# RMS norm and projection on one core: pairs 12 to 14 moved into the loop's order, a new order for the head, output tiles in the weight tile, the last product in two halves

## The chip, the cores and the metric

The kernel runs on one core of one Trainium2 chip. The metric is the device time of one execution in microseconds, the median of several runs. A core has five engines that work side by side, each with its own instruction stream in a fixed order: TensorE (PE: matmuls and transposes, written to the eight banks of PSUM), VectorE (DVE), ScalarE (ACT), GpSimd (POOL) and SyncE (SP, which here issues DMA transfers). They wait for one another through semaphores.

## What is computed

```python
batch, n_heads, seq, head_dim = 8, 12, 1024, 64
dim = n_heads * head_dim                                  # 768
# x: (8, 1024, 768) float32; gamma: ones; w_qkv: (768, 2304) float32
def reference(x, gamma, w_qkv, eps):
    rms = np.sqrt(np.mean(x ** 2, axis=-1, keepdims=True) + eps)
    x_norm = x / rms * gamma
    return np.matmul(x_norm, w_qkv).astype(np.float32)
```

So 8192 rows of 768 are normalised and multiplied with a 768 x 2304 matrix.

## The kernel before, in words

The 8192 rows are 64 tiles of 128 rows. Tiles 0 to 3 are multiplied in the plain way: `mm` (L516) multiplies one 128 x 128 block of the transposed tile with 512 (at the end 256) columns of the bf16 weights, six times for a sum over 768. The other tiles are taken in pairs (pair p is tiles 2p and 2p+1, so pairs 2 to 31), and each pair is multiplied by a scheme of seven products in place of eight. The pair's 256 x 768 input is seen as 2 x 2 blocks, a chunk of 768 weight columns as 2 x 2 blocks of 384 x 384, and `product(p, c, i)` (L686) is product i of pair p and chunk c (0 to 2): three matmuls of 384 columns. The scheme needs four sums of input blocks for each pair (`osum`, L666, on DVE or POOL) and four differences of weight blocks for each chunk (`tsum`, L624, once for all pairs). Weights and inputs of this part are float16; the weights are scaled by a bound that `bound`, `fold`, `bound_tr`, `bound_top`, `bound_all` and `scales` find for each chunk. `bound_tr` and `bound_all` are small PE instructions with a small DVE instruction, `bound_top` (L590), between them.

The seven products of a chunk go to three PSUM banks, named a (products 1, 6, 7, 4 one after the other, added up in the bank), b (product 2) and c (5 and 3). Between two products on one bank its content is read out: `hold` (L693 on DVE, L695 on ACT) copies a bank to a buffer `pp`; `join` (L704, DVE) adds a bank to such a buffer and writes one of the four output quarters; `last` (L708, ACT) writes the fourth. PE can't go on with a bank until its reader is done. `pstore` (L714) sends an output tile of 128 x 768, or half of it, to DRAM.

A tile comes in by `load_x` (L437). In the plain part DVE casts it (`cast`), PE transposes it (`tr`, L480) and DVE or ACT copies the result to `xT` (`cp`); ACT computes the mean square (`stat`). In the pair part, `pstat` (ACT), `prms` (ACT) and `precip` (DVE) find the factor of each row, `pcast` (DVE, L648) writes the normalised tile in float16, and it is transposed either by a DMA (`pxbar`, on SP) or by PE and a copy (`ptr`, `pcp`). Weights come in 16 pieces (`load_w`, L442), which `conv` (L448 on DVE, L450 on ACT, L452 on POOL) converts to the bf16 weight tile `w_b`; `quad` makes the scaled float16 blocks from it. When all 12 of these blocks are made, `w_b` is not read again.

The order of all instructions is written out by hand. `PLAN` (from L19) is a list of 1028 operations with a time for each, and everything up to pair 14 is in it; `STEADY = 15` is the first pair of the loop at the end of the kernel, which gives each operation of pairs 15 to 31 a time in units of `SLOT` (0.4875, the time of one product) after `HEAD_END`. All operations are sorted by that time, and each engine gets its instructions in the order that results. The times are only keys for sorting; loop and list are mixed where their times overlap. In the list of before, pairs 13 and 14 are interleaved with each other, a product of one after a product of the other, and the products of pair 13 go on after `HEAD_END`.

Each kind of buffer comes from a pool of fixed size: 12 tiles `ot` for outputs, 6 `pp`, 4 `xb`, 10 `xT`, 3 sets of input sums, 8 PSUM banks. An instruction that writes into a buffer waits until the readers of what was in it are done, for an output tile until its store has landed.

Of the kernel before, what the change touches and what calls it, by code (L numbers as in the profile page):

```python
# [15 lines left out]
HEAD_END = 165.20  # L16
# [3 lines left out]
    (0.000, "load_x", 2), (4.040, "stat", 2), (4.041, "cast", 2, "DVE"), (4.042, "load_x", 1), (5.240, "stat", 1),  # L20
    (5.241, "load_x", 3), (5.242, "cast", 1, "DVE"), (5.243, "load_x", 0), (5.530, "recip", 2), (5.531, "load_w", 4),
    (5.532, "load_w", 1), (5.533, "load_w", 0), (5.534, "gamma_in"), (5.535, "idle", 6, 512), (5.536, "tr", 2),
    (8.470, "conv", 4, 5, "POOL"), (8.471, "cp", 2, "DVE"), (8.472, "cast", 3, "DVE"), (9.150, "conv", 1, 2, "POOL"),
    (9.151, "tr", 1), (9.152, "tr", 3), (9.153, "recip", 1), (9.154, "cast", 0, "DVE"), (9.155, "cp", 1, "ACT"),
    (9.156, "tr", 0), (9.157, "load_w", 3), (9.158, "cp", 0, "DVE"), (9.310, "mm", 1, 0, "5"), (9.311, "stat", 3),
    (9.526, "mm", 2, 0, "5"), (9.742, "mm", 0, 0, "5"), (9.743, "load_w", 2), (9.744, "load_w", 6),
    (9.745, "recip", 3), (9.990, "mm", 0, 0, "2"), (10.206, "mm", 1, 0, "2"), (10.451, "conv", 0, 0, "DVE"),
    (11.111, "conv", 3, 4, "DVE"), (11.112, "stat", 0), (11.113, "conv", 0, 1, "ACT"), (11.231, "bound", 0, 0, "ACT"),
    (11.541, "recip", 0), (11.772, "conv", 2, 3, "DVE"), (12.202, "cp", 3, "DVE"), (12.203, "mm", 1, 0, "01"),
    (12.204, "mm", 0, 0, "4"), (12.205, "mm", 2, 0, "4"), (12.206, "load_w", 7), (12.207, "mm", 1, 0, "4"),  # L30
    (12.342, "mm", 0, 0, "3"), (13.092, "conv", 6, 2, "DVE"), (13.093, "load_w", 5), (14.413, "conv", 7, 4, "POOL"),
    (14.414, "bound", 0, 1, "DVE"), (14.415, "mm", 1, 0, "3"), (14.416, "mm", 2, 0, "3"), (14.417, "load_w", 9),
    (14.418, "load_w", 8), (14.419, "conv", 6, 3, "ACT"), (14.420, "mm", 0, 0, "01"), (14.421, "mm", 2, 0, "012"),
    (14.422, "mm", 3, 512, "23"), (15.093, "conv", 7, 5, "POOL"), (15.094, "mm", 0, 512, "23"),
    (15.095, "mm", 1, 512, "23"), (15.096, "evac", 0, 0, "ACT"), (15.097, "load_w", 10), (15.098, "load_x", 4),
    (15.734, "conv", 5, 0, "DVE"), (17.054, "conv", 9, 3, "POOL"), (17.055, "evac", 1, 0, "ACT"),
    (17.056, "conv", 5, 1, "ACT"), (17.057, "bound", 0, 2, "ACT"), (17.734, "conv", 9, 2, "POOL"),
    (17.735, "bound", 1, 0, "DVE"), (18.414, "conv", 8, 1, "POOL"), (18.415, "mm", 3, 0, "012345"),
    (18.416, "mm", 1, 512, "45"), (18.417, "fold", 0), (18.418, "mm", 1, 512, "01"), (18.419, "mm", 3, 512, "01"),
    (18.420, "mm", 3, 512, "45"), (18.421, "load_x", 5), (18.544, "bound_tr", 0), (18.545, "evac", 1, 512, "ACT"),  # L40
    (18.664, "mm", 0, 512, "54"), (19.095, "mm", 0, 512, "01"), (19.096, "load_w", 15),
    (19.097, "evac", 3, 512, "ACT"), (19.098, "conv", 8, 0, "POOL"), (19.099, "bound_top", 0),
# [326 lines left out]
def kernel(  # L369
# [319 lines left out]
    def hold(p, c, bank, name, eng):  # L689
        o = PART[p, c, name] = parts.tile([P, CW], f32, name="pp")  # L690
        pb = PB[p, c, bank][:, :CW]
        if eng == "DVE":
            nc.vector.tensor_scalar(out=o, in0=pb, scalar1=SC[c], scalar2=None, op0=mult)  # L693
        else:
            nc.scalar.activation(out=o, in_=pb, func=AF.Copy, scale=SC[c], bias=0.0)  # L695

    def result(p, c, i, j):
        t = 2 * p + i
        if (t, "s", c) not in OUT:
# [107 lines left out]
```

## Time and profile before

| | us |
|---|---|
| three runs | 355.93, 356.56, 357.06 (median 356.56) |
| the profiled execution | 356.93 |
| its span, first to last instruction | 354.8 |
| PE busy | 343.6 |
| DVE busy | 267.8 |
| ACT busy | 243.7 |
| POOL busy | 116.9 |

The mean granted clock of TensorE was 0.995. The durations that matter, by group of instructions: a join 613 ns on DVE, a hold 616 on DVE and 582 on ACT, `last` 577 on ACT, `pcast` 678 on DVE, a weight difference 785 on DVE, an input sum 925 to 938 on POOL. A DMA store of 384 KB takes a median of 4.6 us to land, one of 192 KB 2.3 us. The DMA queues moved 117.8 MB, 332 GB/s over the span.

In a line of the timeline or chain, the first number is the start in us from the first instruction and the second how long it took; "pm L686 x87" is 87 instructions of line 686 that write the tile pm (PSUM). Square brackets give the idle time of that engine just before, and what ended it. In a table of stretches, each column is the busy time of PE, PE's weight loads, DVE, ACT and POOL in that stretch with the number of instructions in brackets, then the granted clock, the busy share of the DMA engines and GB/s.

### The profile page before, as it was taken

What the parts mean: (1) busy time and instruction counts of PE and PEld (TensorE: products, weight loads), DVE (VectorE), ACT (ScalarE), POOL (GpSimd) and SP (SyncE); (2) the same over time, 40 slices, a digit from 0 to 9 for tenths busy, and PEclk for the clock granted to TensorE, in tenths of its full rate; (3) what the DMA queues carried; (4) which work ended last, traced back from release to release, by engine and by line L of the source; (5) the groups of instructions that cost most, each with busy time, mean ns of one, the idle gap of its engine ahead of it and who ended that gap; (6) DMA issues with size and microseconds to landing.
All of it is one profiled execution on the core that took longest, in us unless ns stands there. A gap on an engine that the chain in (4) does not pass through costs nothing.

```text
span 354.8 us, 6638 instructions
## 1 busy us (share of the span) xinstructions
PE 343.6 (97%) x2113; PEld 203.6 (57%) x2113; DVE 267.8 (75%) x504; ACT 243.7 (69%) x498; POOL 116.9 (33%) x135
## 2 busy tenths in 40 slices
PE   5999999999999999999899999999999999999995
PEld 2446566666665656655456566565666656566562
DVE  3689999788778878887676868677777867676663
ACT  6798989878885557656457667676767677665543
POOL 0396444222233303650254080613407061444000
PEclk9899999999999999999999999999999999999999
DMA  7999999999998999999999999999999999987565
GB/s 267 389 381 307 360 416 345 400 347 378 324 393 254 303 361 329 282 350 396 320 332 371 255 380 353 366 334 304 365 360 383 333 327 343 313 305 262 208 266 222
DMA packets 80493, 117.80 MB, mean 332 GB/s; under 512 B 43590, under 2 KB 45388, under 8 KB 80460
## 3 DMA queue, kind: packets, MB, share of 16 engines
q1 hardware_dynamic: 80448, 117.40, 99.1%
q8 instruction: 16, 0.26, 0.3%
q14 instruction: 17, 0.14, 0.1%
q10 hardware_dynamic: 12, 0.00, 0.0%
HBM read 32.25 MB, written 75.50 MB: 304 GB/s over the span
## 4 chain that ended last, share of the span: by engine, by line
PE 54%; DVE 1%; ACT 0%; issue 0%
PE pm L686 54%; DVE ot L704 1%; DVE xb L648 0%; ACT ot L708 0%; DVE pp L693 0%
## 5 line engine op out<-in xcount | busy, mean ns | idle before, releaser
L686 PE MATMUL pm<-wq,su 128*128 128x384 f16 x1080 | 204.9, 326 | 0.8 <-DVE ot L704 0.8
L704 DVE SCALAR_TENSOR_TENSOR ot<-pm,sc,pp 128x384 f32<-128x384 f32 x270 | 156.6, 613 | 47.6 <-PE pm L686 42.3
L695 ACT ACTIVATE pp<-pm,sc 128x384 f32<-128x384 f32 x203 | 114.0, 582 | 75.3 <-PE pm L686 71.9
L686 PE MATMUL pm<-wq,xT 128*128 128x384 f16 x810 | 160.9, 326 | 1.7 <-DVE ot L704 1.5
L686 PEld LDWEIGHTS <-su 128*128 128x128 f16 x1080 | 105.2, 98 | 70.1 <-issue 1.2
L686 PEld LDWEIGHTS <-xT 128*128 128x128 f16 x810 | 79.1, 98 | 54.7 <-issue 2.6
L666 POOL TENSOR_TENSOR su<-xT 128x384 f16<-128x384 f16 x51 | 46.3, 925 | 154.3 <-PE pm L686 84.9
L708 ACT ACTIVATE ot<-pm,sc 128x384 f32<-128x384 f32 x90 | 51.8, 577 | 25.5 <-PE pm L686 24.9
L693 DVE TENSOR_SCALAR pp<-pm,sc 128x384 f32<-128x384 f32 x67 | 40.9, 616 | 23.5 <-PE pm L686 23.0
L634 ACT ACTIVATE sq<-x_t 128x768 bf16<-128x768 f32 x60 | 50.3, 838 | 0.1
L648 DVE TENSOR_SCALAR xb<-x_t,rstd 128x768 f16<-128x768 f32 x60 | 40.3, 678 | 0.4
L666 POOL TENSOR_TENSOR su<-su,xT 128x384 f16<-128x384 f16 x27 | 25.3, 938 | 26.5 <-DVE su L666 14.6
L666 POOL TENSOR_TENSOR su<-xT,su 128x384 f16<-128x384 f16 x27 | 25.2, 935 | 10.0 <-DVE su L666 6.7
L516 PE MATMUL pm<-w_b,xT 128*128 128x512 bf16 (+1 forms) x120 | 26.2, 375 | 0.4 <-POOL w_b L452 0.4
L516 PEld LDWEIGHTS <-xT 128*128 128x128 bf16 x120 | 11.8, 101 | 12.5 <-issue 2.7
L452 POOL TENSOR_SCALAR w_b<-wq,g_sb 128x512 bf16<-128x512 f32 (+1 forms) x14 | 9.1, 662 | 14.0 <-DMA wq<-in_w_qkv_dram 14.0
L618 POOL TENSOR_SCALAR wq<-w_b,inv 128x1152 f16<-128x1152 bf16 x9 | 11.2, 1261 | 4.9 <-DVE inv L602 4.9
L634 ACT ACTIVATION_READ_ACCUMULATOR sq<-x_t 128x1 f32 x60 | 11.7, 195 | 0.0
L624 DVE TENSOR_TENSOR wq<-wq 128x1152 f16<-128x1152 f16 x12 | 9.2, 785 | 0.0
L573 DVE TENSOR_REDUCE bnd<-w_b 128x1 f32<-128x1536 bf16 x5 | 8.7, 1747 | 0.3 <-ACT w_b L450 0.3
L638 ACT ACTIVATE rms<-ssq,eps_sb 128x2 f32<-128x2 f32 x30 | 8.8, 294 | 0.0
L534 ACT ACTIVATE ot<-pm,rstd 128x512 f32<-128x512 f32 x10 | 6.6, 684 | 1.1 <-PE pm L516 1.0
(48 smaller groups left out, 79.3 us busy)
## 6 DMA issues: line engine op xcount, KB each, us to landing
out_dram<-ot SPq DMA_DIRECT2D x178, 384.0 KB, 4.6
x_t<-in_x_dram SPq DMA_DIRECT2D x64, 384.0 KB, 5.4
wq<-in_w_qkv_dram SPq DMA_DIRECT2D x10, 512.0 KB, 9.1
out_dram<-ot SPq DMA_DIRECT2D x8, 512.0 KB, 9.3
wq<-in_w_qkv_dram SPq DMA_DIRECT2D x4, 256.0 KB, 6.8
xT<-xb SPq DMA_TRANSPOSE x49, 5.0
wq<-in_w_qkv_dram SPq DMA_DIRECT2D x2, 384.0 KB, 9.7
out_dram<-ot SPq DMA_DIRECT2D x4, 192.0 KB, 2.3
```

The costliest lines, as they stand in the source:

```text
L452: nc.gpsimd.tensor_scalar(out=o, in0=i, scalar1=g, scalar2=1.0, op0=mult, op1=mult)
L516: nc.tensor.matmul(out=PM[t, n0][:, :nl], lhsT=XT[t][:, ko, :], rhs=w_b[:, ko, n0:n0 + nl], start=(b == 1), stop=(b == KO))
L618: nc.gpsimd.tensor_scalar(out=o, in0=quad_view(c, q), scalar1=INV[c], scalar2=1.0, op0=mult, op1=mult)
L624: (nc.vector if eng == "DVE" else nc.gpsimd).tensor_tensor(out=new_quad(c, q), in0=i0, in1=i1, op=sub)
L634: nc.scalar.activation(out=sq, in_=X[t], func=AF.Square, accum_out=SS[p][:, t % 2:t % 2 + 1])
L648: nc.vector.tensor_scalar(out=XB[t], in0=X[t], scalar1=SS[t // 2][:, t % 2:t % 2 + 1], scalar2=None, op0=mult)
L666: (nc.vector if eng == "DVE" else nc.gpsimd).tensor_tensor(out=block(p, q), in0=block(p, x), in1=block(p, y), op=op)
L686: nc.tensor.matmul(out=PB[k][:, :CW], lhsT=block(p, a)[:, ko, :], rhs=WQ[c, b][:, ko, :], start=(first and ko == 0), stop=(ko == KO // 2 - ...
L693: nc.vector.tensor_scalar(out=o, in0=pb, scalar1=SC[c], scalar2=None, op0=mult)
L695: nc.scalar.activation(out=o, in_=pb, func=AF.Copy, scale=SC[c], bias=0.0)
L704: nc.vector.scalar_tensor_tensor(out=result(p, c, i, j), in0=PB[p, c, bank][:, :CW], scalar=SC[c], in1=PART[p, c, held], op0=mult, op1=add)
L708: nc.scalar.activation(out=result(p, c, 1, 0), in_=PB[p, c, "a"][:, :CW], func=AF.Copy, scale=SC[c], bias=0.0)
```

## The change

The list `PLAN` is replaced by another. It holds the same 1028 operations; about eighty of them stand on another engine (DVE, ACT or POOL) than before, and nearly all have another place. `HEAD_END` is 169.75 in place of 165.20; `STEADY` stays 15. In the new list pairs 12, 13 and 14 follow one another, with the products of a pair in the order that the loop uses, each chunk's products 7 and 4 among the first products of the next chunk. The third chunk of pair 4 stood in the list's times 131 to 142 among pairs 10 to 12; now its seven products are spread from 149 to 173, the last three of them around the first products of the loop. The two kernels' starts, shortened:

```diff
 PLAN = [
-    (0.000, "load_x", 2), (4.040, "stat", 2), (4.041, "cast", 2, "DVE"), (4.042, "load_x", 1), (5.240, "stat", 1),
-    (5.241, "load_x", 3), (5.242, "cast", 1, "DVE"), (5.243, "load_x", 0), (5.530, "recip", 2), (5.531, "load_w", 4),
-    (5.532, "load_w", 1), (5.533, "load_w", 0), (5.534, "gamma_in"), (5.535, "idle", 6, 512), (5.536, "tr", 2),
+    (0.000, "load_x", 1), (1.160, "load_x", 3), (4.040, "stat", 1), (4.041, "cast", 1, "DVE"), (4.042, "load_x", 2),
+    (4.043, "gamma_in"), (4.044, "idle", 6, 512), (5.030, "cast", 3, "DVE"), (5.031, "load_w", 2), (5.260, "tr", 1),
+    (5.820, "cp", 1, "DVE"), (5.821, "stat", 3), (6.820, "stat", 2), (6.821, "load_w", 3), (6.822, "load_x", 0),
+    (6.823, "tr", 3), (6.824, "load_w", 4), (7.480, "conv", 2, 3, "POOL"), (7.481, "load_w", 1),
+    (7.482, "cast", 2, "DVE"), (7.483, "tr", 2), (8.141, "conv", 3, 4, "ACT"), (8.142, "cp", 2, "DVE"),
+    (8.320, "mm", 1, 0, "3"), (8.660, "mm", 2, 0, "3"), (8.921, "mm", 1, 0, "4"), (9.131, "stat", 0),
+    (10.331, "cp", 3, "ACT"), (10.332, "mm", 2, 0, "4"), (10.333, "conv", 4, 5, "POOL"), (10.334, "cast", 0, "DVE"),
+    (10.335, "tr", 0), (10.631, "mm", 2, 0, "5"), (10.847, "mm", 1, 0, "5"), (10.848, "load_w", 0),
...
-    (51.670, "product", 3, 2, 2), (51.671, "tsum", 2, "t2", "DVE"), (52.488, "hold", 3, 2, "a", "p1", "ACT"),
-    (58.464, "product", 4, 0, 6), (58.465, "tsum", 2, "t4", "DVE"), (58.466, "join", 2, 2, 1, 1, "a", "p5"),
+    (51.967, "tsum", 2, "t1", "DVE"), (51.968, "tsum", 2, "t2", "POOL"), (51.969, "pcast", 9),
+    (59.829, "pstore", 3, 1, 0), (59.830, "tsum", 2, "t4", "POOL"), (59.831, "product", 4, 0, 5),
```

And the seam of the list and the loop:

```diff
-    (163.257, "hold", 13, 1, "a", "u2", "DVE"), (163.742, "product", 13, 1, 7), (164.229, "product", 14, 2, 2),
-    (164.632, "join", 13, 1, 1, 1, "a", "p5"), (164.717, "product", 14, 1, 7), (165.204, "product", 14, 2, 6),
-    (165.404, "join", 14, 1, 1, 1, "a", "p5"), (165.692, "product", 14, 2, 3),
-    (166.179, "product", 13, 2, 6), (166.867, "hold", 13, 2, "a", "u2", "ACT"), (166.868, "product", 13, 1, 4),
...
-    (171.054, "product", 13, 1, 3), (171.254, "last", 13, 2), (171.742, "join", 13, 1, 0, 1, "c", "u2"),
+    (169.265, "product", 14, 1, 4), (169.618, "join", 14, 2, 0, 1, "c", "u2"), (169.953, "last", 14, 1),
+    (170.308, "pstore", 14, 2, 0), (170.728, "pstore", 14, 1, 1), (170.729, "product", 14, 2, 7),
+    (170.730, "join", 14, 2, 1, 1, "a", "p5"), (170.731, "product", 4, 2, 2), (170.732, "product", 4, 2, 4),
+    (170.990, "join", 4, 2, 0, 0, "b", "p1"), (171.215, "product", 14, 2, 4), (171.415, "last", 4, 2),
+    (172.055, "pstore", 4, 2, 1), (172.056, "last", 14, 2), (172.057, "product", 4, 2, 3),
```

Output tiles: from pair 4 on, the outputs of chunk 2, and in even pairs also those of chunk 1 of the second tile, are written into slots of `w_b`, nine slots of 768 float32 used in turn. The last chunk of the last pair: product 4 is done as two products of 192 columns, the first half is written out by DVE and stored by SP, the second half by ACT and stored from ACT's queue.

```diff
+    spare = []
     def result(p, c, i, j):
         t = 2 * p + i
         if (t, "s", c) not in OUT:
-            OUT[t, "s", c] = outp.tile([P, 1024], f32, name="ot")
+            if p >= 4 and (c == 2 or (c == 1 and i == 1 and p % 2 == 0)):
+                s = 2 * CW * (len(spare) % (KO * N // (4 * CW)))
+                spare.append((t, c))
+                OUT[t, "s", c] = w_b.rearrange("p k n -> p (k n)").bitcast(f32)[:, s:s + 2 * CW]
+            else:
+                OUT[t, "s", c] = outp.tile([P, 1024], f32, name="ot")
         return OUT[t, "s", c][:, CW * j:CW * (j + 1)]
...
+    def end_piece(p, c, h):
+        w = CW // 2
+        k = (p, c, "a")
+        a, b = PRODUCTS[4]
+        for ko in range(KO // 2):
+            nc.tensor.matmul(out=PB[k][:, w * h:w * (h + 1)], lhsT=block(p, a)[:, ko, :], rhs=WQ[c, b][:, ko, w * h:w * (h + 1)],
+                             start=False, stop=(ko == KO // 2 - 1), skip_group_check=True)
+
+    def end_out(p, c, h):
+        w = CW // 2
+        t = 2 * p + 1
+        o, pb = result(p, c, 1, 0)[:, w * h:w * (h + 1)], PB[p, c, "a"][:, w * h:w * (h + 1)]
+        if h == 0:
+            nc.vector.tensor_scalar(out=o, in0=pb, scalar1=SC[c], scalar2=None, op0=mult)
+        else:
+            nc.scalar.activation(out=o, in_=pb, func=AF.Copy, scale=SC[c], bias=0.0)
+        n0 = 2 * CW * c + w * h
+        (nc.sync if h == 0 else nc.scalar).dma_start(out=of[t * P:(t + 1) * P, n0:n0 + w], in_=o)
...
                 when(9.6, pstore, p, c, 0, 0)
-                when(9.7, last, p, c)
-                when(10.6, pstore, p, c, 1, 0)
+                when(8.5, end_piece, p, c, 0)
+                when(8.6, end_piece, p, c, 1)
+                when(9.7, end_out, p, c, 0)
+                when(9.8, end_out, p, c, 1)
```

In the program that is built, PE raises its semaphore once for the two halves, after the sixth matmul. DVE's output of the first half waits for that count, and ACT's output of the second half waits for DVE's. The orders of DVE, ACT and POOL in the list's part are new; their sums of work are compared in the prediction.

## The prediction

> **What bounds the kernel now.** I read the page first, then busy time in stretches of 10 us, then the chain that ended last, then the timelines of the first 20 us, of 148 to 180 us and of the end.
>
> ```profile
> span 354.8 us, 6638 instructions
> PE 343.6 (97%) x2113; PEld 203.6 (57%) x2113; DVE 267.8 (75%) x504; ACT 243.7 (69%) x498; POOL 116.9 (33%) x135
> ...
> 140.00:150.00 10.00, 10.00 (x63) 6.05 (x62) 8.50 (x17) 7.04 (x16) 5.05 (x6) 1.00 1.16 294
> 150.00:160.00 10.00, 9.51 (x60) 5.59 (x59) 8.69 (x15) 5.49 (x11) 5.98 (x7) 1.00 1.06 336
> 160.00:170.00 10.00, 9.21 (x56) 5.35 (x55) 6.99 (x14) 6.70 (x15) 0.00 (x0) 1.00 1.02 384
> 170.00:180.00 10.00, 9.04 (x56) 5.25 (x54) 7.14 (x12) 3.20 (x6) 3.56 (x4) 1.00 1.13 320
> 180.00:190.00 10.00, 10.00 (x64) 5.99 (x63) 6.86 (x13) 6.73 (x14) 5.76 (x7) 1.00 1.02 362
> ```
>
> TensorE (PE) is the bound. From 20 to 150 us and from 180 to 350 it has no idle time; a full stretch issues 63 or 64 matmuls. Only 150 to 180 falls short (60, 56, 56). The chain says where:
>
> ```profile
> 153.49 14.47 PE pm L686 x87
> ...
> 169.12 0.54 DVE ot L704
> 169.66 0.04 issue
> 169.70 0.66 PE pm L686 x3
> ...
> 170.94 0.63 DVE ot L704
> 171.57 0.04 issue
> 171.62 6.02 PE pm L686 x36
> 177.64 0.02 issue
> 177.66 0.59 ACT ot L708
> 178.25 0.04 issue
> 178.29 171.29 PE pm L686 x1053
> ```
>
> From 178.29 on, 1053 matmuls take 171.29 us: 0.1627 each, 0.488 a product of three. Before that, PE waits for evictions of PSUM banks. An idle mark understates a wait, since a matmul's modelled end lies 0.16 past its slot, so I take starts from the timeline: three matmuls at 152.34 should be followed at 152.83, and the next starts at 153.49 (0.66); likewise 164.69 to 164.85 (0.16), 168.75 to 169.70 (0.95), 170.68 to 171.62 (0.94), 177.95 to 178.29 (0.34). Sum 3.05 us. All five lie in pairs 12 to 14 and their seam with the regular loop.
>
> Two more losses stand at the ends.
>
> ```profile
> 9.38 1.36 POOL L452 TENSOR_SCALAR w_b<-wq,g_sb 128x512 bf16<-128x512 f32 x2 [7.95 <-DMA wq<-in_w_qkv_dram]
> 10.12 10.05 PE L516 MATMUL pm<-w_b,xT 128*128 128x512 bf16 x38 [0.44 <-POOL w_b L452]
> 13.75 5.92 PEld L516 LDWEIGHTS <-xT 128*128 128x128 bf16 x28 [0.24 <-issue]
> 350.27 0.65 PE L686 MATMUL pm<-wq,xT 128*128 128x384 f16 x3 [0.22 <-DVE ot L704]
> 350.96 0.58 ACT L708 ACTIVATE ot<-pm,sc 128x384 f32<-128x384 f32 x1 [1.27 <-PE pm L686]
> ```
>
> The first real matmul waits until 10.12 for weights; up to 13.7 the weight loads of 128x512 matmuls follow 0.43 us apart, after that 0.216: half clock, about 1.8 us lost. At the end, the last product waits 0.38 for a join of its bank (349.89 to 350.27), then come 0.69 to ACT's output, 0.58 for it, and a store.
>
> [...]
>
> **The change, part by part.** The instructions of the head are the same in number: the list of operations differs only in engines and order. Only the last product changes on PE, from three matmuls to six of half width[...]. Sums are against the profiled execution, 356.93 us (span 354.8 and 2.1 around it); the median shown is 0.37 lower, and I subtract that at the end.
>
> *Pairs 12 to 14 in the regular pattern, loop start moved behind them.* In the built order I counted PE work between a product that fills a bank and the instruction that overwrites it. The end of the old kernel gives the price: product at 348.92, join 349.61 to 350.23, next writer 350.27. So 0.86 us of other PE work must lie between; 0.49 lay there and 0.38 was lost. In the old head two places have too little: 0.00 (the 0.94 wait) and 0.49 (the 0.34). The other three have 0.97 or 1.46, with DVE or ACT queued behind casts of x and holds. In the new order nothing from pair 12 to the loop is under 0.97, with the loop's own succession of holds and joins, which from 180 to 349 costs no wait. I count -3.05, and +0.1 for pair 4's third chunk, whose products and joins still sit at the seam.
>
> *Start.* The x order is 1, 3, 2, 0 and two weight pieces come ahead of x 0. Landings by cumulative KB, seen from what waited for them: 384 at 3.85, 768 at 4.82, 1152 at 7.59, 1536 at 8.55, 2560 at 11.33, 3584 at 13.98. In the new order piece 2 ends at 1408 KB: about 8.2, its conversion on POOL 0.69, first matmul 8.9 (before 10.12). But PE then runs out: piece 4 (2304 KB) lands at 10.65 and is ready at 11.4, piece 0 (3072 KB) at 12.65. Between, four matmuls by 10.1, then six at half clock, 11.4 + 6 x 0.43 = 13.97; from there 0.2157 each, so the 30th starts at 13.97 + 19 x 0.2157 = 18.07. Before, 38 are done at 20.10, so the 30th starts at 18.16. Gain 0.1. If the clock stayed full, piece 0 would decide (12.65 + 0.72 + 0.05): gain 0.6. If the window after 13.7 is half too, each such window costs 1.7. I take -0.1. One new wait: the first scale's bound_all now has two matmuls (0.43) behind bound_tr instead of four; transpose 0.22, DVE's 0.28 and two handoffs of 0.06 need 0.62. +0.1; the head's ordinary matmuls queue behind it.
>
> *Rest of the head.* Instructions times mean, by stretches of PE work: from 0 to 50 us of it DVE has 53.9 us (before 54.5), ACT 56.3 (56.7), sums above 50 that the old kernel bore without a wait because neighbours overlap by about 0.06. From 50 to 100 DVE rises from 45.9 to 49.5, ACT falls from 44.1 to 40.3. Tight: the joins of pair 2 behind four weight differences on DVE (trace about 44 to 50), and one join (pair 4, first chunk, bank b) with 0.49 us to the transposes of tile 15 that take a bank; if DVE is free there, 0.38 is lost unless another release hides it. Two weight differences move to POOL, a form that the trace lacks: at least 1.26 (POOL's one-input pass over 1152), at most 3 x 0.925 = 2.78[...]; four sums are queued behind. For all of this +0.4; from 0 to 2.
>
> *Nine output tiles in spent weights.* The old trace shows DVE and ACT waiting for stores of their output tile 0.4 us each in all, outside the chain's PE waits. Nothing. Such a tile waits for the store of nine uses earlier: at five uses in two pairs of 21 x 0.488 = 10.2 us each, over 30 us ago.
>
> *Last product in halves.* PE raises its count once, after the sixth matmul; so DVE's half starts no earlier than the whole did, and ACT's half waits for DVE's. Extrapolated from 256 and 384 columns: DVE 478, 616, so 0.41; ACT 470, 577, so 0.42. From PE's count: 0.41 + 0.05 + 0.42 = 0.88 against 0.58, +0.3. The last store is half as large: stores took 1.8 to 2.8 to land and the end of this one overlaps the drain of those ahead; I take -0.1 (0 to -0.3), while ACT's issue may be slower (0.57 for gamma, 0.33 on SP). Together +0.2, from -0.1 to +0.5. Nothing is queued behind. The 0.38 wait stays.
>
> Sum: -3.05 + 0.1 - 0.1 + 0.1 + 0.4 + 0.2 = -2.35; 356.93 - 2.35 - 0.37 = 354.2.
>
> **Rivals.**
> - *Cleaner*: clock full at the start (-0.6), no wait in the head, the tail even: -3.05 + 0.1 - 0.6 + 0.1 = -3.45, 353.1. For it: PE has 1.2 us of work between 6.9 and 10.3 where it had 0.85. [...]
> - *The head takes it back*: a wait of about 1 us where DVE's differences and joins meet, and others of 0.4 to 0.9 at tile 15 and at POOL's differences: 2.4 instead of 0.4, 356.2. For it: DVE is 9.8 of 10 busy at 40 to 60, and the whole order is new. Against: the old kernel bore the same sums without one wait.
> - *Slower*: the start starves PE between 9 and 13.5 us, and the clock stays half for two windows more, to 20.5. Price 2 x 1.7: 357.6, above the old median. It decides once two windows are lost. For it: from 10.1 to 11.4 PE has six transposes only. Against: from 11.4 PE never stops, and the old kernel warmed after one such window.
>
> **How the numbers follow.** Forecast 0.45 (353.4 to 355.3), cleaner 0.20, head 0.21, slower 0.14. The range 352.9 to 356.5 leaves out the slower case and edges of the others. 0.3% of the median is 1.07 us, about what a measurement of this kernel can tell from no change. Faster than 355.5: cleaner 0.20, forecast 0.43, a quarter of the head case 0.05: 0.68. Slower than 357.6: most of that case, 0.11. Same 0.21.
>
> **What would show it.** Right: all stretches of 150 to 180 with 63 or 64 matmuls; the unbroken PE run begins before 60 us; the 30th ordinary matmul starts near 18.1; ACT's last output starts after DVE's and ends about 1.5 us after the last product's start. Wrong: PE waits on L714 or L718 between 40 and 80 us that sum to over 1.5; half clock after 14 us; a tail shorter than before.

## The result, and the profile after

The changed kernel takes 355.14 us in the median of 4 runs (355.04 to 355.33); the kernel before, run beside it, 356.25 us (355.66 to 357.06). The ratio is 0.9968, with a 95% interval of 0.9946 to 0.9990. Run once more, with 22 runs against 45, it was 355.26 against 356.07 us, ratio 0.998 (0.9967 to 0.9993). So the change is worth 0.8 to 1.1 us, less than half of the 2.35 of the prediction's sum. The profiled execution of the changed kernel took 355.04 us, span 353.0; that of the kernel before 356.93, span 354.8. From one profile to the other that is -1.89 us.

The time lies inside the range on record, 0.9 us above the 354.2 forecast, but the terms are not those of the sum. First the table by stretches of the changed kernel (stretch; its length, busy time of PE and matmuls; granted clock; DMA share; GB/s):

```profile
40.00:60.00 20.00, 19.55 (x132) 1.00 1.03 381
60.00:80.00 20.00, 19.58 (x134) 1.00 1.07 372
80.00:150.00 70.00, 70.00 (x436) 1.00 1.04 341
150.00:160.00 10.00, 9.83 (x62) 1.00 1.09 277
160.00:170.00 10.00, 10.00 (x63) 1.00 1.08 390
170.00:180.00 10.00, 9.59 (x60) 1.00 1.10 329
180.00:340.00 160.00, 160.00 (x987) 1.00 0.98 326
```

The three stretches from 150 to 180 us, which held 9.51, 9.21 and 9.04 us of busy PE before, are almost full: the five old waits are gone. But there are two new ones among them, and two more between 40 and 80 us, where the old kernel had none. The timeline shows what stands ahead of each. First the one at 41.60 us (start; length; engine, line, operation, tiles; in brackets the idle time before and what ended it):

```profile
40.79 1.14 PE L689 MATMUL pm<-wq,su 128*128 128x384 f16 x6
40.99 0.75 DVE L627 TENSOR_TENSOR wq<-wq 128x1152 f16<-128x1152 f16 x1
41.66 0.15 DVE L583 TENSOR_REDUCE bmax<-bnd 128x1 bf16<-128x3 f32 x1
41.72 1.13 DVE L714 SCALAR_TENSOR_TENSOR ot<-pm,sc,pp 128x384 f32<-128x384 f32 x2
...
42.38 0.22 PE L588 MATMUL pm<-ident,bmax 128*1 128x128 bf16 x1 [0.45 <-DVE ot L714]
```

PE's small transpose for the third scale needs a PSUM bank. A join of pair 2 frees it, and DVE comes to that join only at 41.72, behind a weight difference (L627). The last of the six matmuls before it started at 40.79 + 5 x 0.163 = 41.60 and takes 0.163, so 0.62 us are lost by 42.38; 0.09 of that is lost before such a transpose without a wait for a bank too. The other three, in the same view:

```profile
70.55 0.91 POOL L669 TENSOR_TENSOR su<-xT 128x384 f16<-128x384 f16 x1 [3.65 <-DMA xT<-xb]
70.81 1.59 DVE L651 TENSOR_SCALAR xb<-x_t,rstd 128x768 f16<-128x768 f32 x2
71.43 1.14 PE L689 MATMUL pm<-wq,xT 128*128 128x384 f16 x6
72.33 0.61 DVE L714 SCALAR_TENSOR_TENSOR ot<-pm,sc,pp 128x384 f32<-128x384 f32 x1
72.99 0.48 PE L689 MATMUL pm<-wq,su 128*128 128x384 f16 x2 [0.42 <-DVE ot L714]
...
150.28 1.78 POOL L669 TENSOR_TENSOR su<-xT 128x384 f16<-128x384 f16 x2 [2.21 <-PE pm L689]
151.30 1.19 DVE L651 TENSOR_SCALAR xb<-x_t,rstd 128x768 f16<-128x768 f32 x1
153.45 1.63 PE L689 MATMUL pm<-wq,su 128*128 128x384 f16 x9
154.04 0.62 DVE L651 TENSOR_SCALAR xb<-x_t,rstd 128x768 f16<-128x768 f32 x1
154.59 1.13 DVE L714 SCALAR_TENSOR_TENSOR ot<-pm,sc,pp 128x384 f32<-128x384 f32 x2
155.24 0.65 PE L689 MATMUL pm<-wq,xT 128*128 128x384 f16 x3 [0.17 <-DVE ot L714]
...
176.26 0.91 POOL L669 TENSOR_TENSOR su<-xT,su 128x384 f16<-128x384 f16 x1
176.45 1.13 DVE L651 TENSOR_SCALAR xb<-x_t,rstd 128x768 f16<-128x768 f32 x1
177.67 1.67 PE L689 MATMUL pm<-wq,su 128*128 128x384 f16 x9
178.56 0.60 DVE L651 TENSOR_SCALAR xb<-x_t,rstd 128x768 f16<-128x768 f32 x1
179.08 1.66 DVE L714 SCALAR_TENSOR_TENSOR ot<-pm,sc,pp 128x384 f32<-128x384 f32 x3
179.74 0.65 PE L689 MATMUL pm<-wq,xT 128*128 128x384 f16 x3 [0.41 <-DVE ot L714]
```

By starts, from the last matmul of the group before to the next one and less one matmul of 0.163, these are 0.58 us (72.24 to 72.99), 0.33 (154.75 to 155.24) and 0.57 (179.01 to 179.74). In all three a cast of x (L651) stands ahead of the join in DVE's queue, and a cast shortly before took 1.06 to 1.19 us where 0.61 is usual: each time POOL had begun a sum (L669) 0.15 to 0.27 us before it. (In the second group the second sum of the pair is the one that counts: it starts at 151.15.) In this trace 6 of the 60 casts took over 0.8 us, and each ended 0.41 to 0.42 us after the end of the sum that was running when it started (70.55 + 0.91 = 71.46, and the cast at 70.81 took 1.06 and ended at 71.87). What in the chip makes the cast late was not shown.

Start and end of the changed kernel, from the timeline of PE and of the last engines:

```profile
8.66 1.19 PE L519 MATMUL pm<-w_b,xT 128*128 128x512 bf16 x4 [0.57 <-POOL w_b L455]
10.89 1.46 PE L519 MATMUL pm<-w_b,xT 128*128 128x512 bf16 x6 [0.36 <-POOL w_b L455]
12.89 5.99 PE L519 MATMUL pm<-w_b,xT 128*128 128x512 bf16 x26 [0.54 <-ACT w_b L453]
...
348.31 0.66 PE L725 MATMUL pm<-wq,xT 128*128 128x192 f16 x6 [0.22 <-DVE w_b L714]
349.00 0.42 DVE L733 TENSOR_SCALAR w_b<-pm,sc 128x192 f32<-128x192 f32 x1 [0.22 <-PE pm L725]
349.46 0.42 ACT L735 ACTIVATE w_b<-pm,sc 128x192 f32<-128x192 f32 x1 [1.73 <-DVE w_b L733]
```

In this execution no ordinary matmul ran at half rate: six take 1.46 us together. The two halves at the end are evicted one behind the other, as predicted. The sum between the two profiles:

| part | predicted | between the profiles | from |
|---|---|---|---|
| five waits at 150 to 178 gone | -3.05 | -3.05 | starts of matmuls |
| new waits there | +0.1 | +0.90 | 0.33 + 0.57 |
| new waits in the head | +0.4 | +1.20 | 0.62 + 0.58 |
| start, up to 40 us | -0.1 + 0.1 | -1.01 | the rest up to the last product, which starts at 348.31 instead of 350.27 |
| last product's start to the end of the span | +0.2 | +0.19 | 4.71 against 4.52 |
| around the span | 0 | -0.09 | 2.04 against 2.13 |
| sum | -2.35 | -1.86 | -1.89 by the times, the difference is rounding |

### The profile page after: what moved, and what is told of

It reads as the page before. It is cut to its first block, busy times and chain, and to the rows that moved or that the text cites. A ratio compares the mean times of both kernels' runs of the same rounds, so it can differ in the third digit from the quotient of the medians.

```text
span 353.0 us, 6601 instructions
## 1 busy us (share of the span) xinstructions
PE 342.4 (97%) x2113; PEld 203.6 (58%) x2116; DVE 267.1 (76%) x503; ACT 242.6 (69%) x497; POOL 123.5 (35%) x137
## 4 chain that ended last, share of the span: by engine, by line
PE 91%; DVE 3%; DMA 2%; SPq 1%; issue 1%; ACT 0%
PE pm L689 84%; PE pm L519 6%; DMA wq<-in_w_qkv_dram 2%; DVE wq L627 1%; PE pm L674 1%; DVE ot L714 1%; DVE xb L651 1%; SPq L445 1%; SPq L440 0%; DVE xT L459 0%; ACT w_b L453 0%; PE pm L725 0%; DVE w_b L714 0%; DVE su L669 0%; ACT pp L698 0%
## 5 line engine op out<-in xcount | busy, mean ns | idle before, releaser
L714 DVE SCALAR_TENSOR_TENSOR ot<-pm,sc,pp 128x384 f32<-128x384 f32 x172 | 100.2, 612 | 27.0 <-PE pm L689 24.3
L669 POOL TENSOR_TENSOR su<-xT 128x384 f16<-128x384 f16 x50 | 46.1, 938 | 147.0 <-PE pm L689 71.0
L714 DVE SCALAR_TENSOR_TENSOR w_b<-pm,sc,pp 128x384 f32<-128x384 f32 x98 | 58.4, 615 | 23.6 <-PE pm L689 22.4
L651 DVE TENSOR_SCALAR xb<-x_t,rstd 128x768 f16<-128x768 f32 x60 | 39.8, 665 | 0.4
L718 ACT ACTIVATE ot<-pm,sc 128x384 f32<-128x384 f32 x48 | 27.4, 576 | 12.2 <-PE pm L689 11.0
L669 POOL TENSOR_TENSOR su<-xT,su 128x384 f16<-128x384 f16 x28 | 26.2, 936 | 23.1 <-PE pm L689 14.7
L718 ACT ACTIVATE w_b<-pm,sc 128x384 f32<-128x384 f32 x41 | 23.5, 576 | 13.7 <-PE pm L689 13.5
L669 POOL TENSOR_TENSOR su<-su,xT 128x384 f16<-128x384 f16 x26 | 24.9, 958 | 14.3 <-PE pm L689 10.0
L519 PE MATMUL pm<-w_b,xT 128*128 128x512 bf16 (+1 forms) x117 | 25.2, 357 | 1.6 <-POOL w_b L455 0.9
L455 POOL TENSOR_SCALAR w_b<-wq,g_sb 128x512 bf16<-128x512 f32 (+1 forms) x16 | 11.6, 731 | 12.6 <-DMA wq<-in_w_qkv_dram 12.6
L576 DVE TENSOR_REDUCE bnd<-w_b 128x1 f32<-128x1536 bf16 x6 | 10.3, 1748 | 0.6 <-ACT w_b L453 0.3
L621 POOL TENSOR_SCALAR wq<-w_b,inv 128x1152 f16<-128x1152 bf16 x8 | 9.7, 1224 | 1.8 <-DVE inv L605 1.8
L453 ACT ACTIVATE w_b<-wq,g_sb 128x512 bf16<-128x512 f32 (+1 forms) x12 | 7.8, 666 | 3.3 <-DMA wq<-in_w_qkv_dram 3.1
```

Of the source, the lines that this page charges most:

```text
L455: nc.gpsimd.tensor_scalar(out=o, in0=i, scalar1=g, scalar2=1.0, op0=mult, op1=mult)
L519: nc.tensor.matmul(out=PM[t, n0][:, :nl], lhsT=XT[t][:, ko, :], rhs=w_b[:, ko, n0:n0 + nl], start=(b == 1), stop=(b == KO))
L576: nc.vector.tensor_reduce(out=o, in_=v, axis=mybir.AxisListType.XY, op=amax, apply_absolute_value=True)
L621: nc.gpsimd.tensor_scalar(out=o, in0=quad_view(c, q), scalar1=INV[c], scalar2=1.0, op0=mult, op1=mult)
L651: nc.vector.tensor_scalar(out=XB[t], in0=X[t], scalar1=SS[t // 2][:, t % 2:t % 2 + 1], scalar2=None, op0=mult)
L669: (nc.vector if eng == "DVE" else nc.gpsimd).tensor_tensor(out=block(p, q), in0=block(p, x), in1=block(p, y), op=op)
```

## The experiments

Each kernel ran beside the kernel before on the same chip (42, 45 and 27 runs of it in the three groups, medians 355.94, 356.07 and 356.11 us). All of them compute the full output.

### The waits for joins

**Casts one join earlier.** If a sum holds up the cast, the cast should be started ahead of the sum:

```
- when((-45, -57)[odd] + 4.5 * i, pcast, t)
+ when((-45, -57)[odd] + 4.5 * i - {31: 0.98, 36: 0.3}.get(t, 0), pcast, t)
```

> The changed kernel with two casts of x on DVE (tiles 31 and 36) each moved ahead of the one join that stood before it; nothing else on any engine. Theory (a cast waits for a GpSimd sum that started just before it): in the changed kernel these casts took 1.19 and 1.13 us instead of 0.61, started 0.15 and 0.19 us after a sum on POOL, and the PE waits of 0.33 us at 154.75 and 0.57 at 179.01 follow from them. Started one join earlier they are ahead of the sum, take about 0.61, both PE waits go, and the span falls by 0.9 us (0.5 to 1.0). Rival (DVE has too many joins of the held-back chunks in these pairs): the work on DVE is the same in number, so both waits stay within 0.15 us of what they were and the span is unchanged.

Measured: 354.92 us in the median of 9, ratio 0.9973 (0.9960 to 0.9987). The wait at 179 fell from 0.57 to 0.16, that at 154.7 stayed at 0.33. The moved casts met the sum that stood one further ahead: tile 31 took 0.84 us, tile 36 0.95, and now the next cast, tile 32, met a sum too (0.97). Neither theory holds as written. The collision is not removed by moving a cast by one place, since four sums of 0.91 us or more follow one another closely on POOL. The span of 351.9 is only in part the edit's: in this profile the wait at 41 us, which the edit doesn't touch, was 0.11 instead of 0.62.

**The two head waits by order.** A weight difference goes behind the two joins, and a product that opens a bank behind one that does not:

```
- (40.165, "tsum", 1, "t3", "DVE")       (71.862, "product", 5, 1, 5)
+ (41.566, "tsum", 1, "t3", "DVE")       (72.476, "product", 5, 1, 5)
```

The hold that reads this product moved along, from 72.360 to 72.800.

> The changed kernel with the first two waits of the head attacked by order: a weight difference on DVE (chunk 1, t3) moved behind the two joins of pair 2 that stood after it, and on PE product 5 of pair 5, chunk 1 moved behind product 3 of chunk 2. Theory (these are order waits for a join that frees a PSUM bank): the waits of 0.62 us at 41.60 and 0.58 at 72.24 fall to 0.1 or less each, span lower by 1.0 us (0.6 to 1.2). Rival (DVE is simply full there, so that the next instruction in its queue is late instead): waits of the same sum appear within 5 us behind the old places, span unchanged within 0.2.

Measured: 354.73 us in the median of 10, ratio 0.9969 (0.9960 to 0.9978). The first wait is gone (its transpose costs its usual 0.09), the second is 0.15, and nothing came in their place; 0.33 and 0.57 are unchanged. No cast was held up near the second wait in this profile; in three later ones with the same order, where one took 1.27 to 1.34 us, it is 0.28 to 0.36. The theory holds for the waits: about 1.0 us less in the profile. The medians differ by only some 0.5 (354.73 against the 355.26 of the next run), and why they don't show the whole was not settled.

**The changed kernel again.** No edit.

> The changed kernel itself, unedited, beside the others on the same chip. Theory (its waits for joins differ from run to run, because it matters to a fraction of a microsecond which of a DVE pass and a GpSimd sum starts first): the span's waits in the head, 0.62 and 0.58 us in the first profile, come out between 0.1 and 0.8 each; those at 154.7 and 179.0 stay at 0.33 and 0.57; time 355.1 (354.3 to 355.8). Rival (the waits are fixed by the order): all four within 0.05 us of the first profile.

Measured: 355.26 us in the median of 22 (354.19 to 356.81). In this profile the waits are 0.62, 0.83, 0.32 and 0.57. Over the five other profiles that keep the head's order of the changed kernel (the runs with earlier casts, old tail, extra sum, late products and all outputs in ot), the first wait was 0.11, 0.29, 0.15, 0.61 and 0.61, the second 0.78, 0.78, 0.39, 0.75 and 0.42. So the head's waits differ from execution to execution, while 0.33 and 0.57 come back within 0.02 in three of these six profiles. The theory holds in kind; the median time is as expected.

What they differ by can be read in the same profiles. Where one of the weight differences ahead of the first wait took 1.47 us instead of 0.75 (the first profile and three of these), the wait is 0.61 or 0.62. In the three others all of them took 0.75, a sum on POOL beside them took 3.63 us instead of 1.36, and the wait is 0.11, 0.15 and 0.29. The second wait is 0.39 in the profile with the extra sum, where no cast was held up ahead of its join and DVE waited for PE: so much the order costs with DVE free. In the others it follows the cast ahead: 0.42, 0.58, 0.75, 0.78 and 0.83 us where that took 0.90, 1.06, 1.23, 1.27 and 1.32. And the wait at 179 is 0.78 and 1.26 in two profiles, where the cast just ahead of the join was held up too, to 0.82 and 1.30 us: 0.21 and 0.69 more than 0.57, as much as that cast took beyond 0.61. So, with the order unchanged, these two waits of PE grow by as much as a cast on DVE is held up.

**Holds on ACT besides.** With the head reordered, DVE is relieved of one hold ahead of each late join:

```
- (151.941, "hold", 13, 1, "c", "p5", "DVE")
+ (151.941, "hold", 13, 1, "c", "p5", "ACT")
- when(2.1, hold, p, c, "c", "p5", "DVE" if c < 2 else "ACT")
+ when(2.1, hold, p, c, "c", "p5", "DVE" if c < 2 and (p, c) != (15, 1) else "ACT")
```

> The reordering of the two head waits (as in the run of that name: a weight difference behind two joins, one product behind another), and besides the holds of bank c of pairs 13 and 15, chunk 1, on ACT instead of DVE, so that DVE has 0.55 us less to do ahead of the late joins. Theory (PE waits because the join of bank a stands late in DVE's queue; ACT idles 0.9 and 1.4 us there): the waits of 0.33 at 154.7 and 0.57 at 179.0 fall to under 0.1 each; all waits for joins between 40 and 180 us sum to 0.3 or less instead of 2.10; span 351.2 to 351.6, time 354.0 in the median, 1.0 under the changed kernel's. Rival (other instructions become late in their place): the sum stays above 1.0 and the time within 0.4 us of the changed kernel's.

Measured: 353.86 us in the median of 6 (353.54 to 354.18), ratio 0.9936 (0.9920 to 0.9952): 1.4 under the changed kernel beside it. The wait at 179 fell to 0.09. The head kept 0.35 about 72 us and 0.13 at 43, and the wait at 154.4 stayed at 0.32, so that the sum is 0.9 and not 0.3. Why the last of these stayed, the timeline says:

```profile
152.98 0.91 POOL L669 TENSOR_TENSOR su<-xT,su 128x384 f16<-128x384 f16 x1
153.29 1.02 DVE L651 TENSOR_SCALAR xb<-x_t,rstd 128x768 f16<-128x768 f32 x1
...
154.88 0.81 PE L689 MATMUL pm<-wq,xT 128*128 128x384 f16 x4 [0.16 <-DVE ot L714]
```

Without the hold, the cast of tile 32 started earlier, at 153.29, met the sum of 152.98 and took 1.02 us; it ended at 154.31, 0.42 after the sum. The relief was eaten by the 0.41 us that the sum cost the cast.

**The collision by itself.** A needless subtraction on GpSimd is put ahead of a cast in the regular loop, where the changed kernel waits nowhere:

```
+ def extra(p):
+     v = OUT[2 * p, "s", 0][:, :576]
+     nc.gpsimd.tensor_tensor(out=scratch, in0=v, in1=v, op=sub)
...
+ if p % 2 and 17 <= p <= 29 and c == 0:
+     when(6.6, extra, p)
```

> The changed kernel with one needless GpSimd subtraction of 576 f32 columns into a scratch tile in each odd pair from 17 to 29 (seven in all), started by the join that stands two instructions ahead of a cast of x on DVE in the regular loop, where the changed kernel has no PE wait at all; one output buffer fewer makes room for the scratch. Theory (a cast waits for a GpSimd pass that started before it): the seven casts take 0.9 to 1.3 us instead of 0.61, each ends about 0.42 us after the subtraction does, and PE waits of 0.2 to 0.6 us appear before product 4 of chunk 0 in these pairs, together 1.4 to 4 us; span higher by as much. Rival (DVE's own work alone makes joins late): casts at 0.61, no new wait, span unchanged within 0.3.

Measured: 357.27 us in the median of 12, 2.0 above the changed kernel beside it; ratio to the kernel before 1.0031 (1.0015 to 1.0047). The first of them, in pair 17 (the lines of this kernel stand five further down, L694 is the product, L656 the cast, L719 the join):

```profile
198.34 1.15 POOL L635 TENSOR_TENSOR scratch<-ot 128x576 f16<-128x576 f32 x1 [16.58 <-DVE ot L719]
198.73 1.63 PE L694 MATMUL pm<-wq,su 128*128 128x384 f16 x9
198.98 0.93 DVE L656 TENSOR_SCALAR xb<-x_t,rstd 128x768 f16<-128x768 f32 x1
199.83 1.66 DVE L719 SCALAR_TENSOR_TENSOR ot<-pm,sc,pp 128x384 f32<-128x384 f32 x3
200.48 0.81 PE L694 MATMUL pm<-wq,xT 128*128 128x384 f16 x4
```

In the changed kernel, where PE's nine matmuls start at 198.75, the same cast and join read:

```profile
199.00 0.61 DVE L651 TENSOR_SCALAR xb<-x_t,rstd 128x768 f16<-128x768 f32 x1
199.52 1.14 DVE L714 SCALAR_TENSOR_TENSOR ot<-pm,sc,pp 128x384 f32<-128x384 f32 x2
```

The subtraction ends at 199.49, the cast at 199.91; the join behind it starts 0.31 later than the 199.52 of the changed kernel, and PE's nine matmuls, over at 198.73 + 9 x 0.163 = 200.19, are followed at 200.48: a wait of 0.29. All six pairs from 17 to 27 show the same, 0.93 us for the cast and 0.29 for PE, 1.74 together; pair 29 has no cast left at that place, which the expectation overlooked. The rival falls: DVE has not one instruction more. Not all of the 2.0 us is the subtraction's: at 178.3 the profile has 1.26 instead of 0.57, where the cast of tile 37 met a sum and took 1.30. The missing output buffer shows at 47 to 50 us, where DVE waits three times for a store of `ot` (1.5 us), and PE 0.2 us at 50.6; in pairs 17 to 27 nothing waits for a store.

**Casts behind the joins.** Back to holds on DVE; the cast stays in its neighbourhood but no longer stands ahead of the join that PE needs:

```
- when((-45, -57)[odd] + 4.5 * i, pcast, t)
+ when((-45, -57)[odd] + 4.5 * i + {32: 1.45, 37: 0.65}.get(t, 0), pcast, t)
```

> The two reorderings of the head waits, and on DVE the casts of x tiles 32 and 37 each moved behind the join of bank a (pairs 13 and 15, chunk 0) that stood after it; holds back on DVE. Theory (PE waits for a join that stands behind a cast, and casts are what GpSimd's sums hold up): the waits at 154.5 and 178.7 are gone (under 0.1 each), whether or not a cast is held up; time 353.8 (353.4 to 354.2), 1.4 under the changed kernel's. Rival (the holds moved to ACT were what helped): waits as in the changed kernel, 0.33 and 0.57, time 354.7.

Measured: 353.65 us in the median of 5 (353.60 to 354.18), ratio 0.9929 (0.9916 to 0.9942). From its timeline:

```profile
153.37 1.63 PE L689 MATMUL pm<-wq,su 128*128 128x384 f16 x9
154.06 0.62 DVE L714 SCALAR_TENSOR_TENSOR ot<-pm,sc,pp 128x384 f32<-128x384 f32 x1
154.59 0.61 DVE L651 TENSOR_SCALAR xb<-x_t,rstd 128x768 f16<-128x768 f32 x1
154.83 1.46 PE L689 MATMUL pm<-wq,xT 128*128 128x384 f16 x8
...
178.15 0.60 DVE L714 SCALAR_TENSOR_TENSOR ot<-pm,sc,pp 128x384 f32<-128x384 f32 x1
178.68 0.96 DVE L651 TENSOR_SCALAR xb<-x_t,rstd 128x768 f16<-128x768 f32 x1
178.81 1.14 PE L689 MATMUL pm<-wq,xT 128*128 128x384 f16 x6
```

Both waits are gone, although casts were held up as before (1.18 us at 151.22, 1.14 at 176.04, 0.96 at 178.68): 153.37 + 9 x 0.163 = 154.84, and PE goes on at 154.83. Of the changed kernel's 2.10 us of waits 0.28 is left, at 72.9. The theory holds, and this is 2.5 us under the kernel before, about what the forecast had promised of the change itself. No run takes the hold-up of the casts at 151.3 and 176.5 away and leaves the order as it is; that these two hold-ups are needed for the waits of 0.33 and 0.57 is argued from the timeline.

### The start

**The kernel before with more work for PE.** In the profile before, the granted clock is 0.50 for 3.4 us, from about 10.3 to 13.7, and 1.00 on both sides of it:

```profile
9.00:10.00 1.00, 0.51 (x6) 1.00 1.06 404
10.00:10.50 0.50, 0.38 (x2) 0.79 1.07 401
10.50:11.00 0.50, 0.50 (x3) 0.50 1.04 389
11.00:12.00 1.00, 1.00 (x4) 0.50 1.04 387
12.00:13.00 1.00, 1.00 (x4) 0.50 1.05 387
13.00:13.60 0.60, 0.60 (x3) 0.50 1.05 389
13.60:14.00 0.40, 0.40 (x3) 0.87 1.04 384
14.00:15.00 1.00, 1.00 (x6) 1.00 1.05 389
```

This stretch is the window of the prediction, whose price of 1.7 us is an estimate, half of the 3.4; that others would follow at 13.7 was an assumption. The theory here is that more work for PE ahead of 10.3 keeps the clock full after it. Tile 3's six transposes are written five times over instead of once. They ran from 8.06 us on, not at 6.8 as the expectation says, still ahead of 10.3.

```
- for ko in range(KO):
+ for ko in list(range(KO)) * (5 if t == 3 else 1):
```

> The kernel before with 24 more transposes of x tile 3 behind its own six, the same values written again, in the gap of 6.8 to 8.2 us where PE waits for the next tile. Theory [...]: the matmuls after 10.3 follow 0.216 us apart instead of 0.43 when weights are there, mean clock 1.000 instead of 0.995, the 30th ordinary matmul starts at 17.0 to 17.6 instead of 18.07, and the span falls by 0.5 to 1.1 us. Rival (the half window comes from something else): matmuls 0.43 apart as before, span unchanged within 0.2.

Measured: 355.90 us in the median of 14, ratio 0.9996 (0.9982 to 1.0011). In the profile no matmul is at half rate, the 30th ordinary matmul starts at 17.14 instead of 18.07 and the last product at 349.38 instead of 350.27. None of the 14 runs has a mean clock at or under 0.995; of the kernel before beside it 16 of 42 have. So the clock came out as the theory had it, and the price didn't: over runs, the median is unchanged. The runs of the kernel before with a mean clock of 0.999 or 1.000 have a median of 355.61, those at or under 0.995 of 356.17, so that a mean clock at or under 0.995 goes with about 0.6 us; why the kernel with the extra transposes at full clock is no faster than the mixture was not settled.

**The changed kernel with less work for PE.** Its first four ordinary matmuls move from 8.3 to 10.4:

```
- (8.320, "mm", 1, 0, "3"), (8.660, "mm", 2, 0, "3"), (8.921, "mm", 1, 0, "4") ... (10.332, "mm", 2, 0, "4")
+ (10.336, "mm", 1, 0, "3"), (10.337, "mm", 2, 0, "3"), (10.338, "mm", 1, 0, "4") ... (10.339, "mm", 2, 0, "4")
```

> The changed kernel with its first four ordinary matmuls, which run at 8.2 to 9.7 us, moved behind the transposes of x tile 0 (to about 10.4), so that PE has 0.9 us less work between 6.9 and 10.3. Theory [...]: half clock, 0.43 us between matmuls, from about 10.3 to 13.7 in half or more of the runs (mean clock 0.995 or lower), and these runs 0.5 to 1.0 us longer than those at full clock. Rival (the clock doesn't depend on that work): mean clock at or under 0.995 in no more than a quarter of the runs; the span grows only by what the four matmuls lose by starting late, 0.2 us or less.

Measured: 356.69 us in the median of 12, ratio 1.0004 (0.9985 to 1.0023), 1.4 above the changed kernel beside it. The mean clock was at or under 0.995 in 6 of 12 runs (median 356.69), and 0.999 or higher in only two (354.49 and 354.64). The profile has half rate from 10.4 to 15.5 us; the granted clock is 0.50 from about 8.9 to 15.7, 6.8 us instead of the 3.4 of the kernel before. The changed kernel has a mean clock at or under 0.995 in 7 of 22 runs, with a median of 355.61 against 355.12 for those at 0.999 or higher. So the count is the half of the runs that was expected, but 6 of 12 against 7 of 22 is a weak difference; the median and the long stretch at half rate in the profile speak for it more plainly. The price is larger than expected, with only two runs on one side.

So the -1.01 of the first pair of profiles is luck in part. In the second profile of the changed kernel ten ordinary matmuls ran at half rate and the first ordinary one started at 9.35 instead of 8.66; it reached the first head wait 1.54 us later (43.14 against 41.60). That is 0.5 us worse than the profile of the kernel before, not 1.0 better.

### The end and the output tiles

**Old tail in the changed kernel.** The last product is whole, evicted by ACT and stored by SP, as in the lines that the change removed.

> The changed kernel with the last product whole again, as before the change: three matmuls, one output on ACT, one store on SP. Theory (the halves cost what the prediction's sum says, two evictions one behind the other): span lower by 0.2 us (0.0 to 0.5), and the time from the last product's start to the end of the span 4.53 instead of 4.69. Rival (the halves gain, since the last store is half as large): span higher by 0.2 us or more.

Measured: 355.13 us in the median of 22, ratio 0.9984 (0.9973 to 0.9995): no difference that the times can tell. In the profile, 4.64 us from the last product's start to the end of the span, against 4.71; the 4.53 of the theory was not reached.

**No output tiles in spent weights.** `result()` always takes a buffer of `ot`:

```
- if p >= 4 and (c == 2 or (c == 1 and i == 1 and p % 2 == 0)):
-     ...
- else:
-     OUT[t, "s", c] = outp.tile([P, 1024], f32, name="ot")
+ OUT[t, "s", c] = outp.tile([P, 1024], f32, name="ot")
```

> The changed kernel without the nine output tiles in spent weights: every output goes to the twelve output buffers again. Theory (they are worth nothing, since engines hardly waited for a store of an output tile before): time and span within 0.3 us of the changed kernel's (355.26), waits of DVE and ACT for stores of ot together under 1 us and none of them ahead of a PE wait. Rival (the new order leans on them): waits for stores of several us on DVE or ACT, new PE waits, time up by 0.5 us or more.

Measured: 355.33 us in the median of 20, ratio 0.9981 (0.9970 to 0.9993). The waits table has one wait of DVE for a store of `ot`, 0.4 us, and none of ACT. The nine tiles are worth nothing, as predicted. At the end they cost: with the halves in `ot` the last product's start is 4.53 us from the end, with the halves in spent weights 4.70 to 4.77 in eight profiles. Without halves it is 4.52 (two profiles of the kernel before, one with the warm start) against 4.64 or 4.65 (three with spent weights). Why a store from there ends 0.12 to 0.18 later was not found out.

**Casts behind joins and the old tail.**

> As the run with casts behind joins, and the last product whole again (old tail). Theory (the halves cost 0.1 to 0.2 us): median lower by 0.15 us (0.0 to 0.3) than with the halves, and from the last product's start to the end of the span 4.5 to 4.6 us instead of 4.7. Rival (the halves gain): median higher by 0.15 or more.

Measured: 353.58 us in the median of 5 (352.77 to 354.08), ratio 0.9922 (0.9908 to 0.9937); 4.64 us from the last product's start, against 4.71. The medians differ by 0.07: the size is 0.07 by the profiles, too small for the times.

**And a warm start.** Transposes of tile 3 twice and of tile 2 three times over, in the manner of the warm kernel before.

> As the run with the old tail, and transposes of x tiles 3 and 2 written two and three times over with the same values (18 more), in the gaps of PE's first 9 us. Theory [...]: matmuls 0.43 us apart after 8 us become rare, mean clock at or under 0.995 in less than one run in eight (changed kernel: 7 of 22), median lower by 0.3 us (0.0 to 0.6) than without. Rival (the extra transposes delay the first matmuls by as much as the clock gains): median within 0.15 us of that without, or higher.

Measured: 353.36 us in the median of 6, but from 352.90 to 355.22; ratio 0.9929 (0.9908 to 0.9949). None of 6 has a mean clock at or under 0.995 (3 of 5 without). The gain in time is open: too few runs for their spread.

The kernel with the head reordered, casts behind joins and the old tail, 353.58 us, is 2.5 us faster than the kernel before and about 1.7 faster than the changed one.

## Why the prediction came out as it did

*The total: inside the range, in part by luck.* Over the runs the change is worth 0.8 to 1.1 us, and the sum had 2.35. Between the profiles the sum comes out at -1.86 only because the start gave 1.0 us that it did not have, and that the second profile of the changed kernel doesn't have either; the new waits, at the seam and in the head, cost 0.8 each beyond their terms. Of the signs, the end came as said: ACT's output behind DVE's, done at 349.88, 1.57 us after the last product's start. Three did not come: full stretches from 150 to 180 us (62, 63 and 60 matmuls), an unbroken run of PE from before 60 us (it begins at 179.74), and the 30th ordinary matmul near 18.1 (ten stand ahead of 12.89, so it is at 12.89 + 19 x 0.2157 = 16.99).

*The direction and the old waits: right.* All five waits of 150 to 178 us are gone, by starts of matmuls. That the trace's own gaps were the bound was right. But the unbroken run of PE begins later than before, at 179.74 instead of 178.29, behind one of the new waits.

*The new order of pairs 12 to the loop: wrong.* The step that failed reads "nothing from pair 12 to the loop is under 0.97, with the loop's own succession of holds and joins, which from 180 to 349 costs no wait". I counted PE's work between a product and the overwriter of its bank, and took 0.97 as enough because the price was 0.86. For product 4 behind product 7 of pairs 13 and 15 it is exactly 2 x 0.488 = 0.97, so 0.11 is all the room there is, and 0.86 was the price with DVE free. Here a cast stands ahead of the join on DVE, and some casts ahead are held up by half a microsecond. The reading of the old waits had the warning: three of the five places had 0.97 or 1.46, "with DVE or ACT queued behind casts of x and holds", and waited all the same. The term was +0.1 (for pair 4's third chunk), it measured 0.90. The runs show its parts: taking the cast from ahead of the join removes both waits, and lengthening six casts by 0.32 us in the undisturbed loop makes six waits of 0.29.

*The head: right in place, wrong in size.* The weight differences and joins of pair 2 on DVE, and the join of pair 4, first chunk, bank b, were named as the tight spots, and both waited: 0.62 and 0.58 in the first profile against +0.4 for everything. For the second the step had "if DVE is free there, 0.38 is lost", and 0.39 is what the one profile with DVE free there shows. The waiter was another in each case (the transpose of the third scale, and product 5 of pair 5, chunk 1, not the transposes of tile 15). I left out that DVE's durations aren't constant: the weight difference at 38.65 took 1.47 us instead of 0.75, beside a sum on POOL, and the cast at 70.81 1.06 instead of 0.61. The two differences moved to POOL took 2.61 and 2.68 us, inside the step's estimate of 1.26 to 2.78 from other passes in the trace, and PE waited for neither.

*The start: wrong for this profile, and not one number.* The step took half clock from 10.3 to 13.7 as given. Its gain of 0.1 was none: it set the 30th ordinary matmul of the kernel before at 18.16, and that started at 18.07, the very time the sum gives for the changed kernel. In the profile the clock stayed full, which the "cleaner" rival priced at 0.6; it gave 1.0 with the earlier weights. Over runs it is a mixture: half-rate matmuls show in 7 of the 14 profiles of this study, the kernel before among them. That PE's work ahead of 10.3 us has a part in the clock after it fits the runs: a mean clock at or under 0.995 came plainly less often with more of that work (0 of 14 against 16 of 42), weakly more often with less (6 of 12 against 7 of 22); by what rule the clock is granted was not shown. The price of 1.7 us for 3.4 us at half clock was too high for the kernel before, where a mean clock at or under 0.995 goes with 0.6. The wait for `bound_all`, priced at 0.1, did not come: PE loses 0.10 us ahead of it, as in the kernel before. Ahead of `bound_tr`, at 18.5 us, it loses 0.07 more than usual, for DVE's maximum.

*The end: right in its order, and in its sum by luck.* ACT's half waited for DVE's, as said. +0.2 was predicted for the halves and +0.19 measured between the profiles; but the halves cost only 0.01 (4.53 against 4.52, with output tiles in `ot`) to 0.07 (4.71 against 4.64, in spent weights). The rest, 0.12 to 0.18, is the output tile in spent weights, which was priced at nothing. On PE the six matmuls of 192 columns took 0.66 us together, the three of 384 columns before 0.65.

*The base.* The sum was set against one execution of 356.93 us and reduced by 0.37, to a median of three runs. Over 114 further runs the kernel before has medians of 355.9 to 356.1: the execution stood 0.8 to 1.0 above, in part because its clock was at half from 10.3 to 13.7 us. This is the rest between -1.89 from profile to profile and the 0.8 to 1.1 of the medians.

*The rivals.* None came alone: the start was that of the "cleaner" one, the head half way to "the head takes it back" (1.2 of its 2.4 us).

## What to carry to other kernels

- Room between a product and the next writer of its bank must be counted in two queues: PE's work between them, and what stands ahead of the evicting instruction on its own engine, with the longest time that each of these takes, not the mean (for a cast here 1.32 us, not 0.67).
- Put what frees a bank ahead of work that nobody waits for soon. Moving two casts behind two joins removed both waits, of 0.33 and 0.57 us; relieving the engine of two holds removed one of them.
- Before a sum is set against one profiled execution, see where that execution stands among many runs, and how much of it is chance at the start.

## What was not expected of the hardware

A DVE cast of 128 x 768 from f32 to f16 takes 0.61 us, and up to 1.3 us when it meets a GpSimd sum; whenever a held-up cast began, it ended 0.41 to 0.42 us after the sum. POOL pays too: sums that took 0.91 us alone took 1.23 beside a cast, and one beside four weight differences in a row took 3.63. Which of the two is held up is not always what the recorded starts say: at 25.63 us of the changed kernel a cast began 0.11 us after a GpSimd conversion (L455) and took 0.60, while the conversion, 256 columns, took 0.98 instead of the 0.47 that one without a neighbour took.

The record of the granted clock doesn't show every half rate. In the second profile of the changed kernel, the weight loads of 128x512 matmuls between 12.9 and 14.2 us follow 0.43 us apart:

```profile
12.93 0.15 PEld L519 LDWEIGHTS <-xT 128*128 128x128 bf16 x1 [0.28 <-issue]
13.36 0.15 PEld L519 LDWEIGHTS <-xT 128*128 128x128 bf16 x1 [0.28 <-issue]
13.78 0.15 PEld L519 LDWEIGHTS <-xT 128*128 128x128 bf16 x1 [0.28 <-ACT w_b L453]
```

The table by stretches of the same execution has a clock of 1.00 there:

```profile
12.00:15.00 3.00, 3.00 (x9) 1.00 1.05 390
```

Nine matmuls in 3 us instead of fourteen: the distance of matmuls is the surer sign. The mean clock of this execution, 0.997, comes from its last 2 us, where the record has 0.50 and PE has nothing to do. Of the seven profiles with half-rate matmuls three have 0.997 and four 0.995 or less, so the counts of runs by mean clock given above are too low as counts of how often PE ran at half rate.
